# A two-layer hybrid encoder: shares put into the turning matmul, the solve's block products in four lots, the projections in four PSUM banks

## The chip, the core and the metric

The kernel runs on one core of a Trainium2 chip. A core has five engines that work side by side, each on a program of its own that it takes in order: TensorE (PE, matmuls into PSUM), VectorE (DVE), ScalarE (ACT), GpSimd (POOL) and SyncE (SP), which here issues nearly all DMA transfers. PSUM, where matmuls put their sums, has eight banks of 128 partitions x 512 fp32 numbers; all PSUM tiles of this kernel are one or two banks. The metric is device time in microseconds for one call, the median of several runs; lower is better.

## The reference

The input is 512 tokens of 1024 channels. Each of two layers adds half a SwiGLU block (width 2816), a hybrid mixer and another half SwiGLU block to the stream. The mixer projects the normed stream once and feeds three branches: dense attention (4 query heads on 2 key heads, rotary), a mixture of three dilated windows with a learned bias (6 heads; the kernel does it as one softmax with the bias and the logarithm of how many windows hold a key), and a bidirectional gated delta rule (6 heads).

```
def hybrid_mixer(h, rel_bias, w_in, ..., w_out):
    proj = h @ w_in
    aq, ak, av, bq, bk, bv, cq, ck, cv, cz, cb, ca = jnp.split(proj, IN_SPLITS, axis=-1)
    aq = apply_rope(rms_norm(aq, a_qn), cos, sin)          # per head of 64
    ak = apply_rope(rms_norm(ak, a_kn), cos, sin)
    out_a = dense_gqa(aq, ak, av)                          # softmax(q k^T / 8) v
    out_b = dilated_mixture(rms_norm(bq, b_qn), rms_norm(bk, b_kn), bv, rel_bias)
    out_c = gated_deltanet_bidir(cq, ck, cv, cz, cb, ca, c_conv, c_A_log, c_dt_bias, c_out_norm)
    return jnp.concatenate([out_a, out_b, out_c], axis=-1) @ w_out

def gated_delta_chunked(q, k, v, g, beta):                 # chunks of 64 tokens, both directions
    gc = jnp.cumsum(g, axis=-1)
    decay = jnp.where(tril, jnp.exp(gc[..., :, None] - gc[..., None, :]), 0.0)
    M = jnp.where(strict, einsum('bhnid,bhnjd->bhnij', k * beta, k) * decay, 0.0)
    T = triangular_solve(eye + M, eye)                     # one 64x64 inverse per chunk, head, direction
    u, w = T @ (v * beta), T @ (k * beta * jnp.exp(gc))
    a_intra = einsum('bhnid,bhnjd->bhnij', q, k) * decay
    def step(state, xs):                                   # 8 chunks, one after the other
        v_new = u_i - w_i @ state
        o = (q_i * jnp.exp(g_i)) @ state + a_i @ v_new
        state = state * jnp.exp(g_last) + (k_i * jnp.exp(g_last - g_i)).T @ v_new
    ...

def reference(x, ...):
    h = x
    for l in range(DEPTH):                                 # 2
        h = h + 0.5 * swiglu(rms_norm(h, ffn1_norm[l]), ...)
        h = h + hybrid_mixer(rms_norm(h, mix_norm[l]), ...)
        h = h + 0.5 * swiglu(rms_norm(h, ffn2_norm[l]), ...)
    return h
```

In the delta branch q, k and v pass a convolution of five taps and SiLU first, q and k are L2-normed, and the result is normed and multiplied by SiLU(cz).

## The kernel before, in words

**Layout and products.** Channels stand on partitions, the 512 tokens in the free dimension. The large products use fp32r operands split in two: an input `raw` becomes `hi` (rounded, by ScalarE) and `lo` = raw - hi (VectorE), and `mm3` (lines 214 to 218) adds three matmuls, hi by hi, hi by lo, lo by hi. Weights stream from DRAM through two `wraw` buffers; `weight` (line 200) issues the load on SP (line 209), the `whi` copy (210) and the `wlo` subtraction (211).

**Who sets the order.** The source is written as if in sequence. The framework puts all instructions through a scheduler that simulates time and so decides in which order each engine takes its instructions, subject to data, to buffers that must come free, to `issue_after` (this instruction not before that one) and `high_priority`. A pool with `bufs=n` hands out n tiles in turn; a new tile waits for the last reader of the tile whose place it takes. So a change of buffer numbers or of waits moves instructions on every engine.

**The mixer's front** (`mixer`, lines 319 to 366). Two PSUM pools are open while the delta branch is prepared: `mmc` on the right side (three `mm` banks for the projections of q, k and v of the delta branch, `pc`, and one `pss`), and `aux` with four banks on the left for small products: `pR` (line 550, scale rows spread over partitions), `pgq` (614, the 64x64 products of keys and queries per chunk and head) and `pt` (560, 576, transposes; the last reader is the copy to `vs` on ScalarE at 576). Then `aux` and `mmc` close; `join` opens with three banks on the left and `mm` with five on the right (`nmm = 5`), of which four are the former `mmc` banks and one a former `aux` bank. From `mm` come the z projection (`project_z`, 72 matmuls `pc`) and the four group projections (`project_groups`, `pgr`, lines 806 to 808), the group 0 for the dense branch and 1 to 3 for the dilated one. `scales` and `rotate` (from 830 and 858) do the rotary part on VectorE.

**The solve** (`delta_solve`, 623 to 651). The diagonal 32x32 blocks of all 64x64 systems are brought through DRAM into `Z` (96 partitions, both directions; lines 638 and 639, on SP), the reverse direction by way of `zt`. Then 30 rounds r of one multiply into `ztmp` (648) and one add (650) on VectorE, each dependent on the one before. `solve_end` stores the inverses and loads them back into `Y` and `X` (659 to 672). `join_blocks` (683) makes the off-diagonal blocks from them with two sets of 96 matmuls of 32x32 on TensorE, each set in two halves (`pp1`, ScalarE copy `p1s`, `pp2`, four ScalarE copies back to `Y`).

**The attention** (`attention`, from 919) runs in 20 units, five head pairs by four blocks of 128 queries. `scores` of a unit are four matmuls `psc` (954, 955), a row maximum or minimum on VectorE (962, or 966 with the bias), the exponential with its row sum on ScalarE (968, or 963 without the bias), a reciprocal (969) on VectorE, and the multiply by it on GpSimd (970). `weigh` of the unit before (`AHEAD = 1`) turns the probabilities with eight transposes `ppt` (980), copies them on ScalarE (`pth`, 982) and multiplies with v (`pav`, 986). The join is written after the first unit and not issued before its last exponential; then two tables decide: `SCAN_AT` names the units (counted from 0) after which the eight steps of `delta_scan` are written (a step: `pkq`, `prr`, `pS`, `po` on TensorE with VectorE and GpSimd steps between), `FINISH_AT` the unit of `delta_finish`, the output norm of the delta branch (from 1004).

Four lines that the change touches:

```
pt = pp.tile([P, T], F32, name="ppt", tag="t", bufs=2)
for kt in range(NT):
    nc.tensor.transpose(out=pt[:, kt * P:kt * P + P], in_=pb[:, kt * P:kt * P + P], identity=ident)
nc.gpsimd.tensor_tensor(out=pb, in0=pb, in1=sm.to_broadcast([P, T]), op=ALU.mult)
```

Of the kernel before, what the change touches and what calls it, by code (L numbers as in the profile page):

```python
# [9 lines left out]
F32 = mybir.dt.float32  # L10
# [19 lines left out]
SCAN_AT = (1, 3, 4, 6, 7, 9, 10, 12)  # L30
FINISH_AT = 13
# [81 lines left out]
class Body:  # L113
# [205 lines left out]
    def mixer(self, n, l, sm, nxt):  # L319
# [4 lines left out]
        with scope("mix") as mp:  # L324
# [7 lines left out]
            with scope("qkv") as qkvp:  # L332
# [8 lines left out]
                m.nmm = 5  # L341
# [11 lines left out]
                with self.tc.issue_after(m.exps[-1].ins):  # L353
                    m.join_blocks(pool)
                m.square_group(0)
                unit = next(units)
                solve.__exit__(None, None, None)
# [20 lines left out]
class Mixer:  # L378
# [23 lines left out]
    def conv(self, pp, pool, ct):  # L402
# [10 lines left out]
        for j in range(1, 5):  # L413
            nc.vector.scalar_tensor_tensor(out=y, in0=xb[:, j:j + T], scalar=w(j), in1=y, op0=ALU.mult, op1=ALU.add)
# [112 lines left out]
    def delta_keys(self, pool, cs, pss):  # L527
# [16 lines left out]
        nc.vector.tensor_tensor(out=both[32:64], in0=rows[0:32], in1=both[0:32], op=ALU.subtract)  # L544
# [78 lines left out]
    def delta_solve(self, pool):  # L623
# [10 lines left out]
        zt = pool.tile([n96, 32, 32], F32, name="zt", tag="zt")  # L634
# [7 lines left out]
        tmp = pool.tile([n96, 2, 256], F32, name="ztmp", tag="zt")  # L642
# [40 lines left out]
    def join_blocks(self, pool):  # L683
        nc, X = self.nc, self.X
        parts = []
        for hf in range(2):
            for d in range(2):
                a, b = 64 * hf + 32 * d, 64 * hf + 32 * (1 - d)
                parts.append((self.Y[d], slice(a, a + 32), slice(b, b + 32), slice(32 * (1 - d), 32 * (1 - d) + 32)))
        turns = [(q, divmod(q, 6)) for q in range(12)]  # L690
        for tp in range(2):
            p1 = self.aux("pp1")
            for q, (t, h) in turns:
                t += 2 * tp
                for y, ra, rb, cols in parts:
                    nc.tensor.matmul(out=p1[rb, q * 32:q * 32 + 32], lhsT=y[ra, t, h, cols], rhs=X[ra, t * 6 + h],
                                     start=True, stop=True)
            ps = pool.tile([P, 384], F32, name="p1s")
            nc.scalar.activation(out=ps, in_=p1[:, 0:384], func=AF.Copy)
            p2 = self.aux("pp2")  # L700
            for q, (t, h) in turns:
                t += 2 * tp
                for y, ra, rb, cols in parts:
                    nc.tensor.matmul(out=p2[ra, q * 32:q * 32 + 32], lhsT=ps[rb, q * 32:q * 32 + 32],
                                     rhs=y[rb, t, h, cols], start=True, stop=True)
            for y, ra, rb, cols in parts:
                dst = y[ra, 2 * tp:2 * tp + 2].rearrange("p t h i -> p (t h) i")[:, :, cols]
                nc.scalar.activation(out=dst, in_=p2[ra, 0:384].rearrange("p (q i) -> p q i", i=32), func=AF.Copy)
# [210 lines left out]
    def attention(self, ap, pp):  # L919
# [18 lines left out]
        def scores(tile_, t):  # L938
# [18 lines left out]
            for par in range(2):  # L957
# [6 lines left out]
                else:  # L964
# [3 lines left out]
                    nc.scalar.activation(out=pb, in_=pb, func=AF.Exp, scale=-1.0, bias=nm, accum_out=sm)  # L968
                nc.vector.reciprocal(out=sm, in_=sm)  # L969
                nc.gpsimd.tensor_tensor(out=pb, in0=pb, in1=sm.to_broadcast([P, T]), op=ALU.mult)  # L970
                probs.append(pb)
            return probs, state["pv"], v, tile_, t

        def weigh(probs, pv, v, tile_, t):
            tk = slice(t * P, t * P + P)
            turns = []
            for pb in probs:
                pt = pp.tile([P, T], F32, name="ppt", tag="t", bufs=2)
                for kt in range(NT):
                    nc.tensor.transpose(out=pt[:, kt * P:kt * P + P], in_=pb[:, kt * P:kt * P + P], identity=ident)  # L980
                full = ap.tile([P, T], F32, name="pth", bufs=4)
                nc.scalar.activation(out=full, in_=pt, func=AF.Copy)
                turns.append(full)
# [155 lines left out]
```

## Time and profile before

| | |
|---|---|
| median of 3 runs | 2235.09 us (2233.28 to 2237.33) |
| profiled execution, its own time | 2239.25 us |
| its span, first to last instruction | 2237.2 us |
| TensorE matmul (PE), weight loads (PEld) | busy 2168.8 us (97%), 1735.0 us (78%) |
| VectorE (DVE) | 1122.6 us (50%) |
| ScalarE (ACT) | 778.5 us (35%) |
| GpSimd (POOL) | 399.7 us (18%) |
| mean granted clock of TensorE | 0.98 |

The profile is one execution recorded by the hardware. Times are microseconds from the span's start, durations of single instructions in ns where the view says so. A granted clock of 1.00 is the full 2.4 GHz, 0.5 is 1.2 GHz. The two feed-forward blocks of a layer fill TensorE; the mixer of layer 0 lies at about 395 to 713 us, that of layer 1 at about 1505 to 1830. PE's share of 97% overstates how full it is, since a record of a pipelined matmul is longer than the distance to the next one. In a timeline a row is: start, duration, engine, line, operation, output<-inputs, tile, how many in a row, and in brackets the idle time before it with what ended it.

### The profile page before, as it was taken

What the parts mean: (1) busy time and instruction counts of PE and PEld (TensorE: products, weight loads), DVE (VectorE), ACT (ScalarE), POOL (GpSimd) and SP (SyncE); (2) the same over time, 40 slices, a digit from 0 to 9 for tenths busy, and PEclk for the clock granted to TensorE, in tenths of its full rate; (3) what the DMA queues carried; (4) which work ended last, traced back from release to release, by engine and by line L of the source; (5) the groups of instructions that cost most, each with busy time, mean ns of one, the idle gap of its engine ahead of it and who ended that gap; (6) DMA issues with size and microseconds to landing.
All of it is one profiled execution on the core that took longest, in us unless ns stands there. A gap on an engine that the chain in (4) does not pass through costs nothing.

```text
span 2237.2 us, 30694 instructions
## 1 busy us (share of the span) xinstructions
PE 2168.8 (97%) x12548; PEld 1735.0 (78%) x12548; DVE 1122.6 (50%) x1787; ACT 778.5 (35%) x1127; POOL 399.7 (18%) x378
## 2 busy tenths in 40 slices
PE   7999999989898999999999999999898999999999
PEld 5888887769776888888788888877697768888887
DVE  5333334688477543333443333347875765333333
ACT  4222223533565422222332222235336643222221
POOL 3101012210253210101121010123004531101010
PEclk9999999979899999999999999999799999999999
DMA  5332323224202233233322323232242032332323
GB/s 174 124 94 93 96 94 122 78 65 116 77 28 86 85 95 95 94 94 94 94 94 87 102 91 98 92 121 73 74 115 59 28 104 91 95 94 93 97 92 99
DMA packets 93524, 206.83 MB, mean 92 GB/s; under 512 B 38626, under 2 KB 39138, under 8 KB 93385
## 3 DMA queue, kind: packets, MB, share of 16 engines
q1 hardware_dynamic: 91616, 199.98, 29.2%
q10 hardware_dynamic: 1768, 4.91, 0.8%
q8 instruction: 98, 1.61, 0.3%
q14 instruction: 42, 0.34, 0.0%
HBM read 193.83 MB, written 14.18 MB: 93 GB/s over the span
## 4 chain that ended last, share of the span: by engine, by line
PE 88%; DVE 7%; ACT 2%; issue 2%; DMA 1%; POOL 1%; SPq 0%; DVEq 0%; ACTq 0%; POOLq 0%
PE pg L218 15%; PE pg L216 15%; PE pg L217 15%; PE pd L218 7%; PE pd L217 7%; PE pd L216 7%; PE pgr L808 2%; PE pgr L807 2%; PE pgr L806 2%; PE pc L216 2%; PE pc L217 2%; PE pc L218 2%; PE pav L986 1%; PE pwo L217 1%; PE pwo L216 1%
## 5 line engine op out<-in xcount | busy, mean ns | idle before, releaser
L210 ACT ACTIVATE whi<-wraw 128x1024 fp32r<-128x1024 f32 (+3 forms) x344 | 351.4, 1022 | 1234.7 <-PE pg L217 667.1
L216 PE MATMUL pg<-xh,whi 128*128 128x512 f32 x1408 | 557.8, 397 | 8.3 <-ACT xh L236 8.1
L217 PE MATMUL pg<-xl,whi 128*128 128x512 f32 x1408 | 558.3, 397 | 2.9 <-DVE xl L237 2.9
L218 PE MATMUL pg<-xh,wlo 128*128 128x512 f32 x1408 | 557.5, 396 | 0.8 <-DVE wlo L211 0.8
L211 DVE TENSOR_TENSOR wlo<-wraw,whi 128x1024 fp32r<-128x1024 f32 (+3 forms) x344 | 408.1, 1186 | 95.5 <-ACT whi L210 88.3
L296 POOL TENSOR_TENSOR s<-s,rstd 128x512 f32<-128x512 f32 x88 | 152.7, 1737 | 1146.5 <-ACT s L295 1146.5
L216 PEld LDWEIGHTS pg<-xh,whi 128*128 128x128 f32 x1408 | 265.1, 188 | 73.0 <-ACT xh L236 8.1
L217 PEld LDWEIGHTS pg<-xl,whi 128*128 128x128 f32 x1408 | 265.1, 188 | 68.5 <-DVE xl L237 5.2
L218 PEld LDWEIGHTS pg<-xh,wlo 128*128 128x128 f32 x1408 | 265.1, 188 | 65.2 <-DVE wlo L211 1.9
L218 PE MATMUL pd<-hh,wlo 128*128 128x512 f32 x704 | 278.7, 396 | 0.9 <-DVE wlo L211 0.9
L216 PE MATMUL pd<-hh,whi 128*128 128x512 f32 x704 | 278.5, 396 | 0.0
L217 PE MATMUL pd<-hl,whi 128*128 128x512 f32 x704 | 278.4, 395 | 0.0
L310 DVE SCALAR_TENSOR_TENSOR x<-pd,x 128x512 f32<-128x512 f32 x96 | 66.3, 691 | 285.2 <-PE pd L218 285.2
L298 DVE TENSOR_TENSOR h<-pg,s 128x512 f32<-128x512 f32 x88 | 60.9, 692 | 287.6 <-PE pg L218 281.1
L294 DVE TENSOR_TENSOR s<-pg,rstd 128x512 f32<-128x512 f32 x88 | 60.5, 691 | 230.4 <-PE pg L218 230.2
L218 PEld LDWEIGHTS pd<-hh,wlo 128*128 128x128 f32 x704 | 132.3, 188 | 34.0 <-DVE wlo L211 2.2
L217 PEld LDWEIGHTS pd<-hl,whi 128*128 128x128 f32 x704 | 132.4, 188 | 31.8
L216 PEld LDWEIGHTS pd<-hh,whi 128*128 128x128 f32 x704 | 132.4, 188 | 31.8
L970 POOL TENSOR_TENSOR prob<-prob,row 128x512 f32<-128x512 f32 x80 | 82.7, 1040 | 107.2 <-DVE row L969 67.1
L245 POOL TENSOR_TENSOR acc<-acc,sq 128x512 f32<-128x512 f32 x42 | 67.4, 1606 | 132.5 <-ACT sq L244 131.9
L216 PE MATMUL pc<-xh,whi 128*128 128x512 f32 (+1 forms) x208 | 85.4, 412 | 5.6 <-ACT vs L576 4.8
L807 PE MATMUL pgr<-wlo,xh 128*128 128x384 f32 (+1 forms) x256 | 89.9, 351 | 0.0
(248 smaller groups left out, 2554.2 us busy)
## 6 DMA issues: line engine op xcount, KB each, us to landing
wraw<-in_gu_dram SPq DMA_DIRECT2D x176, 512.0 KB, 3.6
wraw<-in_wd_dram SPq DMA_DIRECT2D x64, 448.0 KB, 3.4
wraw<-in_wd_dram SPq DMA_DIRECT2D x32, 512.0 KB, 3.5
wraw<-in_w_c_dram SPq DMA_DIRECT2D x24, 512.0 KB, 3.5
wraw<-in_w_gb_dram SPq DMA_DIRECT2D x24, 384.0 KB, 3.1
wraw<-in_w_o_dram SPq DMA_DIRECT2D x14, 512.0 KB, 4.0
bias<-line SPq DMA_DIRECT2D x12, 448.0 KB, 5.2
saved<-x SPq DMA_DIRECT2D x16, 256.0 KB, 2.0
```

The costliest lines, as they stand in the source:

```text
L210: nc.scalar.activation(out=hi, in_=raw, func=AF.Copy)
L211: nc.vector.tensor_tensor(out=lo, in0=raw, in1=hi, op=ALU.subtract)
L216: nc.tensor.matmul(out=out, lhsT=w[0], rhs=x[0], start=first, stop=False)
L217: nc.tensor.matmul(out=out, lhsT=w[0], rhs=x[1], start=False, stop=False)
L218: nc.tensor.matmul(out=out, lhsT=w[1], rhs=x[0], start=False, stop=last)
L245: nc.gpsimd.tensor_tensor(out=n["acc"], in0=n["acc"], in1=sq, op=ALU.add)
L294: nc.vector.tensor_tensor(out=s, in0=p, in1=n["rstd"], op=ALU.mult)
L296: nc.gpsimd.tensor_tensor(out=s, in0=s, in1=n["rstd"], op=ALU.mult)
L298: nc.vector.tensor_tensor(out=h, in0=pp[1], in1=s, op=ALU.mult)
L310: nc.vector.scalar_tensor_tensor(out=self.x[dm], in0=p, scalar=0.5, in1=self.x[dm], op0=ALU.mult, op1=ALU.add)
L807: nc.tensor.matmul(out=o, lhsT=xh[:, tk], rhs=lo[:, wc], start=False, stop=False)
L970: nc.gpsimd.tensor_tensor(out=pb, in0=pb, in1=sm.to_broadcast([P, T]), op=ALU.mult)
```

## The change

1. *Shares in the turning matmul.* The GpSimd multiply of the probabilities (128x512) by the reciprocal of their sums is gone. VectorE makes instead `share`, the identity (128x128) with its rows multiplied by the reciprocals, and `weigh` uses it as the right operand of a plain fp32 matmul with the unnormed probabilities as the left one. A transpose with the identity becomes a matmul with a diagonal; the product is the transposed block with each column scaled.
2. *The join in four lots.* `join_blocks` takes the indices of lots, one per pair of scan steps (token block t forward, 3 - t backward). Each lot is 24 matmuls, one copy, 24 matmuls and four copies, all in one bank `pp`. Lots 0 and 1 are written after the first unit, 2 and 3 after the second; before, all followed the first. `SCAN_AT` and `FINISH_AT` stand up to one unit earlier.
3. *Projections in their former banks.* `nmm` is 4 instead of 5.
4. *Around the solve.* `zt` lives in the place of the first keys (`kh`) and `ztmp` has its own place (they shared one); the VectorE taps of the convolution of `ct == 7` are not issued before the `rqr` subtraction of `delta_keys`.

```
-SCAN_AT = (1, 3, 4, 6, 7, 9, 10, 12)
-FINISH_AT = 13
+SCAN_AT = (1, 2, 3, 5, 6, 8, 9, 11)
+FINISH_AT = 12
@@ mixer
-                m.nmm = 5
+                m.nmm = 4
...
                 with self.tc.issue_after(m.exps[-1].ins):
-                    m.join_blocks(pool)
+                    m.join_blocks(pool, (0, 1))
                 m.square_group(0)
                 unit = next(units)
+                with self.tc.issue_after(m.exps[-1].ins):
+                    m.join_blocks(pool, (2, 3))
@@ conv
-        for j in range(1, 5):
-            nc.vector.scalar_tensor_tensor(out=y, in0=xb[:, j:j + T], scalar=w(j), in1=y, op0=ALU.mult, op1=ALU.add)
+        with self.tc.issue_after(self.last_r.ins) if ct == 7 else nullcontext():
+            for j in range(1, 5):
+                nc.vector.scalar_tensor_tensor(out=y, in0=xb[:, j:j + T], scalar=w(j), in1=y, op0=ALU.mult, op1=ALU.add)
@@ delta_keys
-        nc.vector.tensor_tensor(out=both[32:64], in0=rows[0:32], in1=both[0:32], op=ALU.subtract)
+        self.last_r = nc.vector.tensor_tensor(out=both[32:64], in0=rows[0:32], in1=both[0:32], op=ALU.subtract)
@@ delta_solve
-        zt = pool.tile([n96, 32, 32], F32, name="zt", tag="zt")
+        zt = self.homes[0].tile([n96, 32, 32], F32, name="zt", tag="kh")
...
-        tmp = pool.tile([n96, 2, 256], F32, name="ztmp", tag="zt")
+        tmp = pool.tile([n96, 2, 256], F32, name="ztmp")
@@ join_blocks
-        for tp in range(2):
-            p1 = self.aux("pp1")
...
+        for lot in lots:
+            parts = []
+            for hf in range(2):
+                for d in range(2):
+                    a, b = 64 * hf + 32 * d, 64 * hf + 32 * (1 - d)
+                    t = lot if d == 0 else 3 - lot
+                    parts.append((self.Y[d][:, t], t * 6, slice(a, a + 32), slice(b, b + 32),
+                                  slice(32 * (1 - d), 32 * (1 - d) + 32)))
+            p = self.aux("pp")
+            for h in range(6):
+                for y, x0, ra, rb, cols in parts:
+                    nc.tensor.matmul(out=p[rb, h * 32:h * 32 + 32], lhsT=y[ra, h, cols], rhs=X[ra, x0 + h],
+                                     start=True, stop=True)
+            ps = pool.tile([P, 192], F32, name="p1s", bufs=2)
+            nc.scalar.activation(out=ps, in_=p[:, 0:192], func=AF.Copy)
...
@@ attention
+                share = ap.tile([P, P], F32, name="share", bufs=2 * AHEAD + 2)
                 nc.vector.reciprocal(out=sm, in_=sm)
-                nc.gpsimd.tensor_tensor(out=pb, in0=pb, in1=sm.to_broadcast([P, T]), op=ALU.mult)
-                probs.append(pb)
+                nc.vector.tensor_scalar(out=share, in0=ident, scalar1=sm, scalar2=None, op0=ALU.mult)
+                probs.append((pb, share))
...
-            for pb in probs:
+            for pb, share in probs:
...
-                    nc.tensor.transpose(out=pt[:, kt * P:kt * P + P], in_=pb[:, kt * P:kt * P + P], identity=ident)
+                    nc.tensor.matmul(out=pt[:, kt * P:kt * P + P], lhsT=pb[:, kt * P:kt * P + P], rhs=share,
+                                     start=True, stop=True)
```

What the scheduler makes of it, at three places. First TensorE's program behind the last convolutions of layer 0 (`pc` is a projection, `pR` and `pgq` as above). Before, the small products follow each other:

```order
L217 MATMUL pc<-xl,whi 128x512
L218 MATMUL pc<-xh,wlo 128x512
L550 MATMUL pR<-rqr,pick 128x512 x6
L614 MATMUL pgq<-kq_3123 64x128 x4
L614 MATMUL pgq<-kq_3124 64x128 x4
L614 MATMUL pgq<-kq_3123 64x128 x2
L614 MATMUL pgq<-kq_3124 64x128 x2
L614 MATMUL pgq<-kq_3125 64x128 x6
```

Now, a few rows further on in the same stretch, the z projection's `pc` stands between them:

```order
L218 MATMUL pc<-xh,wlo 128x512
L553 MATMUL pR<-rqr,pick 128x512
L216 MATMUL pc<-xh,whi 128x512
L217 MATMUL pc<-xl,whi 128x512
L218 MATMUL pc<-xh,wlo 128x512
L216 MATMUL pc<-xh,whi 128x512
L217 MATMUL pc<-xl,whi 128x512
L553 MATMUL pR<-rqr,pick 128x512
L617 MATMUL pgq<-kq_3123 64x128 x4
L218 MATMUL pc<-xh,wlo 128x512
L216 MATMUL pc<-xh,whi 128x512
```

The 72 z matmuls, which came behind all `pR`, `pgq` and `pt`, now stand among the `pR` and `pgq`; the `pt` transposes stand among the matmuls of group 0.

Second, SP's queue at the solve of layer 0 (`w_c` is the weights of the delta branch and z, `w_ga` those of group 0, `w_gb` of groups 1 to 3; `Y` forward is 3169, backward 3170). Before:

```order
L209 DMA wraw<-in_w_c_dram 128x1024 x10
L209 DMA wraw<-in_w_ga_dram 128x1024
L638 DMA s_0_0_3464<-Y_3169 32x24x32 x2
L638 DMA s_0_1_3467<-Y_3170 32x24x32 x4
L638 DMA s_0_0_3464<-Y_3169 32x24x32 x2
L639 DMA zt<-s_0_1_3467 96x1024
L639 DMA Z<-s_0_0_3464 96x1024
L209 DMA wraw<-in_w_ga_dram 128x1024 x3
L209 DMA wraw<-in_w_gb_dram 128x768 x5
L662 DMA s_0_0_3465<-Z 96x1024
```

Now:

```order
L209 DMA wraw<-in_w_c_dram 128x1024 x10
L209 DMA wraw<-in_w_ga_dram 128x1024 x3
L641 DMA s_0_0_3464<-Y_3169 32x24x32 x2
L641 DMA s_0_1_3467<-Y_3170 32x24x32 x3
L209 DMA wraw<-in_w_ga_dram 128x1024
L641 DMA s_0_1_3467<-Y_3170 32x24x32
L641 DMA s_0_0_3464<-Y_3169 32x24x32 x2
L642 DMA Z<-s_0_0_3464 96x1024
L209 DMA wraw<-in_w_gb_dram 128x768
L642 DMA zt<-s_0_1_3467 96x1024
L209 DMA wraw<-in_w_gb_dram 128x768 x11
L665 DMA s_0_0_3465<-Z 96x1024
```

Two more `w_ga` loads stand ahead of the first store of `Y`, one load stands among the stores and one between the loads of `Z` and `zt`; the store of the solved `Z` stands behind the last `w_gb` load instead of the fifth.

Third, GpSimd at the start of layer 0's attention (`prob` the multiply that goes, `qkv` the scaling of the dilated groups, `S` the state of the scan). Before:

```order
L671 COPY bias<-Z 96x512 x2
L881 MEMSET kl_4291 64x512
L970 TENSOR_TENSOR prob<-prob,row 128x512 x8
L855 TENSOR_TENSOR qkv_3968<-qkv_3968,rqb 128x256 x4
L970 TENSOR_TENSOR prob<-prob,row 128x512
L855 TENSOR_TENSOR qkv_4097<-qkv_4097,rqb 128x256 x4
L855 TENSOR_TENSOR qkv_4249<-qkv_4249,rqb 128x256 x4
L970 TENSOR_TENSOR prob<-prob,row 128x512
L763 TENSOR_TENSOR S<-S,lstep 128x384
```

Now:

```order
L674 COPY bias<-Z 96x512 x2
L881 MEMSET kl_4291 64x512
L855 TENSOR_TENSOR qkv_3968<-qkv_3968,rqb 128x256 x4
L855 TENSOR_TENSOR qkv_4097<-qkv_4097,rqb 128x256 x4
L855 TENSOR_TENSOR qkv_4249<-qkv_4249,rqb 128x256 x4
L763 TENSOR_TENSOR S<-S,lstep 128x384 x4
L780 TENSOR_TENSOR otok<-otok,t_5173 64x384 x2
L763 TENSOR_TENSOR S<-S,lstep 128x384
```

The twelve `qkv` scalings follow one another, and nothing stands between the scan's state steps but the outputs of the delta branch, `otok`.

On TensorE the first `prr` of the scan stands behind 24 `psc` matmuls instead of 18, that is twelve score pairs instead of nine, and behind the last `po` there are eight `psc` instead of six.

## Rows read from the trace of the kernel before

**Rows 1.** Stage table of layer 0's mixer, a stretch each.

```profile
core 0: us, PE busy (x) PEld busy (x) DVE busy (x) ACT busy (x) POOL busy (x), PEclk, DMA share, GB/s
...
463.00:494.00 31.00, 24.34 (x139) 17.37 (x140) 23.40 (x61) 11.03 (x13) 0.00 (x0) 0.51 0.33 75
...
494.00:555.00 61.00, 61.00 (x299) 53.96 (x298) 56.55 (x114) 19.35 (x27) 0.00 (x0) 1.00 0.39 103
...
581.00:600.00 19.00, 11.40 (x314) 8.08 (x314) 9.06 (x20) 13.49 (x29) 9.20 (x10) 0.73 0.61 170
600.00:690.00 90.00, 84.52 (x1426) 65.85 (x1423) 63.63 (x151) 58.21 (x121) 47.38 (x53) 0.96 0.06 19
690.00:713.00 23.00, 19.11 (x158) 13.28 (x154) 20.36 (x56) 12.53 (x27) 8.21 (x9) 1.00 0.25 80
```

**Rows 2.** Timeline of TensorE, from the convolutions to the first scores.

```profile
460.87 0.39 PE L217 MATMUL pc<-xl,whi 128*128 128x512 f32 x1
461.10 0.40 PE L218 MATMUL pc<-xh,wlo 128*128 128x512 f32 x1
...
463.39 1.48 PE L550 MATMUL pR<-rqr,pick 64*128 64x512 f32 x3 [1.89 <-DVE rqr L544]
...
488.35 0.80 PE L216 MATMUL pc<-xh,whi 128*128 128x512 f32 x1 [2.38 <-ACT vs L576]
...
507.95 0.86 PE L806 MATMUL pgr<-whi,xh 128*128 128x512 f32 x3
...
580.80 0.34 PE L807 MATMUL pgr<-wlo,xh 128*128 128x384 f32 x1
580.98 0.34 PE L808 MATMUL pgr<-whi,xl 128*128 128x384 f32 x1
```

**Rows 3.** Waits of TensorE: us in total, times, longest.

```profile
PE pc L216 <- ACT vs L576: 4.8, 2, 2.4
...
PE pp L696 <- issue: 4.5, 1, 4.5
```

**Rows 4.** Timeline of VectorE: the solve, and the rotation's end.

```profile
492.39 0.22 DVE L648 TENSOR_TENSOR ztmp<-Z 96x60 f32<-96x60 f32 x1 [7.26 <-DMA Z<-s]
...
537.71 0.27 DVE L650 TENSOR_TENSOR Z<-Z,ztmp 96x60 f32<-96x60 f32 x1
...
554.98 0.56 DVE L874 TENSOR_TENSOR qkv<-qkv,rope 128x384 f32<-128x384 f32 x1
```

**Rows 5.** Turning by source line (min/median/max ns), then TensorE's timeline.

```profile
L980 PE MATMUL ppt<-consts,prob x320: 270/273/474, 589.9 to 1812.1; 128*128 128x128 f32 x160
...
640.99 1.04 PE L980 MATMUL ppt<-consts,prob 128*128 128x128 f32 x8
...
1880.45 1.06 PE L261 MATMUL prow<-consts,rcol 128*128 128x128 f32 x8
```

**Rows 6.** Chains of 581 to 713 and of 640 to 662, by line.

```profile
by line: PE pav L986 10.9%; issue 10.7%; PE ppt L980 8.4%; POOL qkv L855 4.6%; PE psc L954 4.6%; PE psc L955 3.5%; DVE prob L966 3.0%; ACT prob L968 3.0%; DMA woraw<-in_w_o_dram 2.7%; PE pqk L887 2.4%; DVE row L962 2.3%; PE po L769 2.3%; PE
...
614.62 4.88 POOL qkv L855 x8
...
by line: PE pav L986 24.4%; PE ppt L980 15.2%; PE psc L954 13.1%; PE psc L955 9.2%; PE pkq L733 7.8%; PE po L769 6.7%; ACT kh L908 6.2%; PE pS L756 5.8%; PE pqk L887 4.7%; PE prr L746 3.8%; ACT pth L982 2.8%; issue 0.8%
```

**Rows 7.** GpSimd's multiply by source line, and its idle time (us, times).

```profile
L970 POOL TENSOR_TENSOR prob<-prob,row x80: 1029/1040/1062, 585.2 to 1810.5; 128x512 f32<-128x512 f32 x80
...
  DVE row L969: 67.1, 42
```

**Rows 8.** VectorE by source line, all calls: min/median/max ns.

```profile
L426 DVE TENSOR_SCALAR half<-small x2: 178/184/189, 6.3 to 717.3; 128x45 f32<-128x45 f32 x2
...
L812 DVE TENSOR_SCALAR qkv<-pgr,rcol x4: 617/618/618, 580.3 to 1690.8; 128x384 f32<-128x384 f32 x4
```

**Rows 9.** Timeline of TensorE at the mixer's end.

```profile
707.19 0.55 PE L1026 MATMUL pot<-consts,otok 128*128 128x128 f32 x3 [0.94 <-DVE otok L1021]
...
709.86 0.66 PE L1026 MATMUL pot<-consts,otok 128*128 128x128 f32 x4 [0.85 <-DVE z L1030]
```

More of the change, by code (lines that the diff above doesn't have):

```diff
@@ L681, in solve_end, with join_blocks @@
         self.X = X
-    def join_blocks(self, pool):
+    def join_blocks(self, pool, lots):
         nc, X = self.nc, self.X
[L685 to L690, printed above, removed]
-        for tp in range(2):
-            p1 = self.aux("pp1")
[L693 to L696, printed above, removed]
-                                     start=True, stop=True)
[L698 to L708, printed above, removed]
@@ new lines, in join_blocks @@
+        for lot in lots:
[10 more added lines that the diff above has]
+                    nc.tensor.matmul(out=p[rb, h * 32:h * 32 + 32], lhsT=y[ra, h, cols], rhs=X[ra, x0 + h],
+                                     start=True, stop=True)
+            ps = pool.tile([P, 192], F32, name="p1s", bufs=2)
+            nc.scalar.activation(out=ps, in_=p[:, 0:192], func=AF.Copy)
+            for h in range(6):
+                for y, x0, ra, rb, cols in parts:
+                    nc.tensor.matmul(out=p[ra, 192 + h * 32:224 + h * 32], lhsT=ps[rb, h * 32:h * 32 + 32],
+                                     rhs=y[rb, h, cols], start=True, stop=True)
+            for y, x0, ra, rb, cols in parts:
+                nc.scalar.activation(out=y[ra, :, cols], in_=p[ra, 192:384].rearrange("p (h i) -> p h i", i=32), func=AF.Copy)
```

## The prediction

> **What bounds the kernel now.** I read the page first: its slices are dense and at full clock but for one dip in each layer's mixer, where the change lies; then the stage table, the timeline, the waits and the chain. The stage table of layer 0 [rows 1] shows three stretches. From 463 to 494 us TensorE's clock is granted at 0.51, that is the lower of its two levels (1.2 of 2.4 GHz), while VectorE is busy 23.40 of 31 us. From 494 to 581 TensorE is dense. From 581 to 713, the attention with the delta scan, nobody is full: in 600 to 690 VectorE has 63.63 of 90 us, ScalarE 58.21, GpSimd 47.38, and TensorE's 84.52 is flattered, since a record is longer than the distance to the next.
>
> What stands behind the first stretch is in TensorE's timeline [rows 2]. The last matmul of the convolutions starts at 461.10; then come only the `pR`, `pgq` and `pt` products, each waiting for VectorE; the z projection (72 matmuls `pc`) starts at 488.35 after 2.38 us on ScalarE's `vs`; the group projections start at 507.95 and the last stands at 580.98. The list of waits has that `vs` wait twice, once per layer [rows 3]. `vs` is the last reader of a bank of the former `aux` pool, so z waits for a PSUM bank, not for data or weights.
>
> **The mixer's front: banks and the order that follows.** With four `mm` buffers the projections take the four banks that `mmc` leaves. The order of instructions shows the result: in TensorE's program the 72 z matmuls stand among `pR` and `pgq`, and the `pt` transposes among the first group matmuls; before, all of these came first. So z fills the time in which TensorE waited. Count, layer 0, from 461.5 (the last convolution matmul issued) to 581.15 (the first score, one matmul behind 580.98), 119.7 us: z at full clock is 72 x 0.233 = 16.8 us (the spacing 460.87 to 461.10); the groups 507.95 to 581.15 are 73.2 us; `pR`, `pgq`, `pt` took 25.0 us (463.39 to 488.35) with waits and at half clock, so their work is 12.5 us at most, and I put it at 10. Sum 100; at best 119.7 - 100 = 19.7 us per layer go away.
>
> What is late next is VectorE. The solve's chain of 60 dependent multiplies and adds runs 492.39 to 537.98, after an idle 7.26 us on the DMA of `Z`, and the rotation ends at 555.5 [rows 4]: 63 us almost dense. In the new order the solve's steps, the rotation and the weight splits `wlo` of the groups share one stretch, so VectorE again needs about 63 us from the first solve step (z's own steps and three large splits leave the stretch, five smaller ones and the first pair's operands come into it, and I count these as equal). On SP's queue three `w_ga` loads now stand ahead of the stores of Y, one among them, and a `w_gb` load ahead of `zt`. That puts the first step at about 499 instead of 492.4 and the end of the solve at 562; the last split is some 5 us earlier (a dozen short steps follow it), and 4.2 us of matmuls (24 at the 0.175 of 580.80 to 580.98 [rows 2]) follow it: projections end at 561 to 563. So I take 18 of the 19.7 us. Bounds: 20.5 (the three small products at 9 us) and 8 (TensorE still falls to half clock for some 20 us of the stretch, or the split paces it). The solve now ends with the projections instead of 43 us before, so the stores of Z and the loads of Y join the DMA chain of `X` on SP; eight turning matmuls that stood behind the join's first product now stand ahead of it on TensorE and cover that wait. I cost it at nothing, and at 3 us if the cover is too short.
>
> Moving `zt` to the place of the first keys and one convolution's VectorE steps behind `rqr` are in the 18: they are what lets `pR` follow the convolutions without the 1.89 us wait.
>
> **The attention: what the turning costs.** A transpose is one TensorE record: eight in 1.04 us, less the last one's 0.273, are 110 ns each. The new turning is a plain fp32 matmul of 128x128 by 128. That form is in the trace: `prow`, four calls, eight records in 1.06 us, so 112 ns a record and two records a call, 224 ns [rows 5]. 160 turnings a layer cost 160 x (0.224 - 0.110) = 18.2 us more of TensorE. The Trainium skill (TensorE: Matmul & The Clock Gate, section Terms) states that the transpose mode is four times faster for FP32. By that a turning would cost 440 ns and the layer 53 us more; the `prow` rows show twice, not four times, and the sum goes by them.
>
> How much of it counts? The chain through 581 to 713 has 8.4% in `ppt`, that is 11.1 us of 132 [rows 6], out of 160 x 0.110 = 17.6 us of transposes: 63%. So +11.5 us. (In 640 to 662 TensorE's lines sum to 91% of the chain: there all of it counts.)
>
> GpSimd loses 40 multiplies of 1.04 us a layer [rows 7]. On the chain the 4.88 us of `qkv` scaling at 614.62 stand between two of them on its in-order queue; the chain gives 4.6% = 6.1 us to `qkv` [rows 6], and the two multiplies at its ends make 2. These 8.1 us go. What is late next is the same stretch's VectorE work (the `rtb` steps and `vn`), so I credit 5.
>
> VectorE gains 40 `share` products of 128x128 a layer. No row has this form: 45 columns take 184 ns, 384 columns out of PSUM 618 [rows 8]; the line between them gives 290 at 128, and I take that, 11.6 us a layer. Bounds: 7.4 us all hidden (40 x 0.184, zero on the path) and 25 (40 x 0.618). VectorE is busy 70% of this stage but its largest line in the chain has 3.0%; I count a quarter, +3.
>
> The join in four lots keeps its 192 products and its copies' elements; its 4.5 us `issue` gap [rows 3] may go or come back; -1. The scan's first step now stands behind twelve score pairs instead of nine, and its last ahead of four instead of three, so eight steps go with 12 units of attention instead of 14. A step so has 1.5 units beside it instead of 1.75, and a unit's eight turnings cost 0.9 us more: the two about cancel. The final norm starts a unit earlier; before, TensorE waited for it at the end, 0.94 and 0.85 us [rows 9], so -2.
>
> Sum of the attention: 11.5 - 5 + 3 - 1 - 2 = +6.5, taken as +6. Bounds: +18.2 + 11.6 = +30 with no credit, and -8 when GpSimd's and the tail's go in full and the rest hides.
>
> **The sum.** Per layer -18 + 6 = -12, two layers -24 us. The profiled execution took 2239.25 (span 2237.2), the median of the runs is 2235.09; the same 24 off both: 2215 profiled, **2211** as a median.
>
> **Rivals.**
> - *GpSimd was the hidden bound.* 67.1 us of GpSimd's idle time are waits for VectorE's reciprocals [rows 7]: the multiply is a serial link between exponential and turning, 1.04 us each. With it gone the attention shortens by 6 instead of growing: -24 a layer, **2187**. Against it: 640 to 662 is a TensorE chain.
> - *The gap is filled only half.* The clock still falls, or the splits pace TensorE: -9 + 6 = -3 a layer, **2229**. For it: VectorE is busy 23.40 of the 31 us and its splits feed TensorE; against it: z waited for no split.
> - *TensorE becomes the attention's bound.* All 18.2 us count, no credits: 0 a layer, **2235**. For it: 640 to 662; against: the `ppt` share over the whole stage.
> - *Slower: the solve paces everything from SP's queue.* The stores of Y stand behind weight loads that wait for `wraw` buffers, each released a period of 24 x 0.233 = 5.6 us later. If three periods are lost, the solve starts 16.8 us late, and since splits and solve share VectorE the projections end as much later: -18 + 16.8 + 6 = +5 a layer, **2245**. It decides from 12 us of delay. Against it: Y is ready about when the buffers come free.
> - *Slower: the turning at four times a transpose*, a longer matmul in the place of `ppt`: 160 x 0.33 x 0.63 = 33 instead of 11.5 us, -18 + 28 = +10 a layer, **2255**; from 0.32 us a turning the change loses. Against it: `prow`. This is the price that the Trainium skill's section Terms gives.
>
> **How the numbers follow.** Forecast 0.48, hidden GpSimd bound 0.20, half filled 0.10, TensorE bound 0.08, SP's queue 0.10, dear turning 0.04. About 0.2%, 4.5 us, is what a measurement of this kernel can tell from no change. Faster than that: 0.47 + 0.20 + 0.09 + 0.03 = 0.79; within it: 0.07; slower: 0.14. The forecast's own range is 2197 to 2225. For 8 in 10 I go down to 2185 (0.08 lie below) and up to 2242, where about 0.11 lie above.
>
> **What would show it.** Right: z's `pc` records between 461 and 485 at full clock, the `vs` wait gone, the first score near 563; `ppt` with 640 records of 112 ns; `share` near 0.29 us; GpSimd without `prob`; the attention from first score to first dense `pwo` 136 to 142 us. Wrong: a first score later than 573, solve steps starting after 505, a `share` over 0.6 us or a turning over 0.3 us; or an attention shorter than 130 us, which would mean that GpSimd's link was the bound.

## The result, and the profile after

The changed kernel takes 2210.47 us, the median of 4 runs (2208.95 to 2210.93), against 2236.21 before. The ratio is 0.9885, with a 95% interval of [0.9868, 0.9902]; the forecast was 2211. The profiled execution took 2210.73 us with a span of 2208.9, that is 28.3 us less than the span before. The medians are 25.7 us apart: the profiled execution before (2239.25 us) lay 3 us above its median, so what the traces say below holds the difference some 2 to 3 us too large.

First the places to which the prediction was tied, TensorE's timeline of the changed kernel (start, duration, what, idle time before in brackets):

```profile
460.84 0.40 PE L218 MATMUL pc<-xh,wlo 128*128 128x512 f32 x1
461.17 1.19 PE L553 MATMUL pR<-rqr,pick 64*128 64x512 f32 x4
462.29 0.51 PE L216 MATMUL pc<-xh,whi 128*128 128x512 f32 x1
...
560.94 0.34 PE L808 MATMUL pgr<-whi,xl 128*128 128x384 f32 x1
561.12 0.39 PE L954 MATMUL psc<-kh,qs 128*128 128x512 f32 x1
```

`pR` follows the convolutions without the wait of [rows 2], z starts 1.1 us behind the first `pR` instead of 25, and the first score stands at 561.12 instead of 581.15. The stage table of the same kernel, layer 0: the old gap, the solve, the attention up to its last turning, and the attention of layer 1:

```profile
core 0: us, PE busy (x) PEld busy (x) DVE busy (x) ACT busy (x) POOL busy (x), PEclk, DMA share, GB/s
461.00:485.00 24.00, 24.00 (x179) 17.92 (x178) 22.03 (x49) 5.51 (x7) 0.67 (x2) 1.00 0.22 73
503.00:561.00 58.00, 57.49 (x324) 55.52 (x324) 55.47 (x119) 23.88 (x38) 2.70 (x3) 1.00 0.27 79
561.00:692.00 131.00, 125.17 (x2024) 103.37 (x2022) 97.80 (x263) 83.29 (x181) 20.83 (x26) 0.99 0.17 47
1655.00:1787.00 132.00, 125.09 (x2021) 102.60 (x2021) 97.43 (x263) 83.08 (x180) 20.82 (x26) 0.99 0.17 46
```

Against [rows 1], the clock of the old gap is 1.00 where it was 0.51, and TensorE is busy in all of it. The attention's own rows before, over the same stretch of work:

```profile
581.00:713.00 132.00, 115.03 (x1890) 87.20 (x1888) 93.05 (x226) 84.23 (x175) 64.79 (x70) 0.94 0.17 51
1691.00:1823.00 132.00, 117.19 (x1899) 88.40 (x1899) 95.58 (x230) 85.29 (x175) 64.80 (x70) 0.95 0.19 60
```

TensorE was busy for 115 us of 132, with the clock at 0.94; now it is busy for 125 of 131, at 0.99. The waits of TensorE in layer 0's mixer, all that are left (us in total, times, longest):

```profile
PE psc L954 <- ACT prob L963: 3.9, 2, 2.1
PE ppt L981 <- DVE qs L897: 1.9, 2, 1.1
PE pwo L216 <- ACT mxh L1033: 0.8, 1, 0.8
PE pgr L806 <- ACT whi L210: 0.4, 1, 0.4
PE pwo L216 <- DVE x L1051: 0.3, 1, 0.3
PE pwo L217 <- DVE mxl L1034: 0.2, 1, 0.2
```

The `vs` wait and the 4.5 us of `pp` [rows 3] are gone. The chain through the attention of layer 0, that is the work followed back from the last instruction of the stretch, is TensorE's (shares by line, and one of its pieces):

```profile
by line: PE ppt L981 29.5%; PE pav L988 19.1%; PE psc L954 7.6%; PE psc L955 6.0%; PE prr L746 4.6%; PE po L769 4.0%; PE pkq L733 3.3%; PE pS L756 2.9%; DMA woraw<-in_w_o_dram 2.8%; DMA s<-bias 2.4%; DVE qs L897 2.3%; PE pp L699 2.1%; ACT q
...
575.63 0.89 PE ppt L981 x8
```

Compared with [rows 6], the turning went from 8.4% to 29.5%, and `qkv` on GpSimd and `issue` (time in which an engine waits for nothing that the profile shows) are no longer among the large ones. Last, VectorE's timeline with the solve's first step, one of its longest and its last, and the two operations whose price was estimated, by source line (min/median/max ns):

```profile
503.33 0.22 DVE L651 TENSOR_TENSOR ztmp<-Z 96x60 f32<-96x60 f32 x1 [8.30 <-ACT Z L644]
...
541.38 0.59 DVE L651 TENSOR_TENSOR ztmp<-Z 96x420 f32<-96x420 f32 x1
...
559.07 0.27 DVE L653 TENSOR_TENSOR Z<-Z,ztmp 96x60 f32<-96x60 f32 x1
```

```profile
L981 PE MATMUL ppt<-share,prob x640: 270/275/377, 564.6 to 1786.7; 128*128 128x128 f32 x160
...
L971 DVE TENSOR_SCALAR share<-consts,row x80: 275/286/1034, 564.3 to 1783.2; 128x128 f32<-128x128 f32 x80
```

**Where the time went, by layer.** Up to the first score, layer 0 is 20.0 us shorter (561.12 against 581.15). From the first score to the first dense matmul of the feed-forward block the attention is 3.3 us longer (561.12 to 738.43 against 581.15 to 755.18). In layer 1 it is -19.0 (738.43 to 1654.82 against 755.18 to 1690.59, the feed-forward blocks between being the same) and +7.9 (1654.82 to 1833.50 against 1690.59 to 1861.35). Together -28 of the span's -28.3.

### The profile page after: what moved, and what is told of

The parts are those of the page before. It is cut to its first block, busy times and chain, and to the rows that moved or that the text cites. A ratio compares the mean times of both kernels' runs of the same rounds, so it can differ in the third digit from the quotient of the medians.

```text
span 2208.9 us, 31208 instructions
## 1 busy us (share of the span) xinstructions
PE 2174.3 (98%) x12868; PEld 1754.8 (79%) x12868; DVE 1130.1 (51%) x1867; ACT 782.1 (35%) x1147; POOL 320.0 (14%) x298
## 4 chain that ended last, share of the span: by engine, by line
PE 91%; DVE 3%; ACT 2%; DMA 2%; issue 1%; POOL 1%; SPq 0%; ACTq 0%; POOLq 0%; DVEq 0%
PE pg L218 15%; PE pg L216 15%; PE pg L217 15%; PE pd L218 7%; PE pd L216 7%; PE pd L217 7%; PE ppt L981 4%; PE pav L988 2%; PE pgr L807 2%; PE pgr L808 2%; PE pgr L806 2%; PE pc L216 1%; PE pc L218 1%; PE pc L217 1%; PE pwo L218 1%; PE pwo L216 1%
## 5 line engine op out<-in xcount | busy, mean ns | idle before, releaser
L981 PE MATMUL ppt<-share,prob 128*128 128x128 f32 x640 | 91.8, 284 | 3.8 <-DVE qs L897 3.8
L981 PEld LDWEIGHTS ppt<-share,prob 128*128 128x128 f32 x640 | 80.1, 191 | 15.3 <-issue 5.8
L808 PE MATMUL pgr<-whi,xl 128*128 128x384 f32 (+1 forms) x256 | 90.0, 353 | 0.0
```

Of the source, the lines that this page charges most:

```text
L808: mm = nc.tensor.matmul(out=o, lhsT=xl[:, tk], rhs=hi[:, wc], start=False, stop=kk == KD - 1)
L981: nc.tensor.matmul(out=pt[:, kt * P:kt * P + P], lhsT=pb[:, kt * P:kt * P + P], rhs=share, start=True, stop=True)
```

## The experiments

The time of the kernel before differs a little from one set of runs to the next, so all figures below are differences of ratios to the kernel before, times 2237 us; "a layer" is half of that. Each interval reaches about 0.0014 to either side, so a difference of two rows is known to about 2.3 us a layer: those of about 3 us are only just clear of it, and those under 1 us tell nothing.

| run | ratio, 95% interval | against | a layer |
|---|---|---|---|
| the changed kernel | 0.9885 [0.9868, 0.9902] | before | -12.9 us |
| e12_nmm | 0.9877 [0.9863, 0.9891] | before | -13.8 |
| e3_around | 0.9993 [0.9984, 1.0002] | before | -0.8 |
| e1_front | 0.9833 [0.9820, 0.9847] | before | -18.7 |
| e2_turn | 1.0048 [1.0034, 1.0062] | e3_around | +6.2 |
| e5_front_turn | 0.9912 [0.9899, 0.9926] | e1_front | +8.8 |
| e6_front_plain | 0.9966 [0.9953, 0.9979] | e1_front | +14.9 |
| e7_front_nomul | 0.9880 [0.9866, 0.9893] | e1_front | +5.3 |
| e9_nomul_held | 0.9837 [0.9821, 0.9853] | e1_front | +0.4 |
| e8_front_dve | 0.9840 [0.9827, 0.9854] | e1_front | +0.8 |
| e11_dve_held | 0.9873 [0.9857, 0.9889] | e8_front_dve | +3.7 |
| e10_noshare | 0.9911 [0.9898, 0.9925] | the changed kernel | +2.9 |
| e4_back | 0.9861 [0.9847, 0.9874] | the changed kernel | -2.7 |

### The front alone

```
-                m.nmm = 5
+                m.nmm = 4
+ zt in the place of the first keys, ztmp a place of its own,
+ issue_after(self.last_r.ins) around the taps of ct == 7
```

> Before with the front parts alone: four projection banks, the two places around the solve, the one convolution's taps held back. The transposes, GpSimd's multiply, the join in two halves and the scan tables stay. My theory: the first score comes about 20 us earlier in each layer and the attention is what it was before, so 2236 - 2 x 19 = 2198 (2194 to 2204). Rival, the gain is handed back: the solve ends with the projections, and without the join in lots the attention waits for it, 4 or more us a layer, 2206 or more. Rival, the front needs nothing but is lengthened by its own splits: 2215 or more.

Measured 2201.08 us: my theory. The first score is at 561.66, the front 19.5 us shorter, and the attention as before (first score to feed-forward block 174.0 us, before 174.0). Nothing was handed back behind it, and this kernel is 0.5% faster than the changed one.

The two places without the bank (the diff above without its first two lines):

> Before with only the two places around the solve and the one convolution's taps held back; five projection banks. The control of the two runs above. My theory: the 1.9 us wait for the scale rows goes at most, 2232 to 2237, since z still waits for its bank. Rival, these places are what lets the front shorten: 2215 or less.

Measured 2236.06, no change that can be told. And the bank without the two places (the first two lines alone):

> Before with four projection banks and nothing else. My theory, the bank is the cause: most of e1_front's gain, 53 of the 72 z matmuls in the gap against 63 there, 2205 (2201 to 2210). Rival, the moved places around the solve are needed as well: 2215 or more.

Measured 2209.91, at the upper edge of the 2201 to 2210 expected: the bank is the main cause, at -13.8 of the -18.7. The other 5 us a layer come from the places, but only once the bank is there. e12_nmm's timeline shows how:

```profile
462.83 0.40 PE L218 MATMUL pc<-xh,wlo 128*128 128x512 f32 x1
465.12 1.18 PE L550 MATMUL pR<-rqr,pick 64*128 64x512 f32 x4 [1.89 <-DVE rqr L544]
466.44 0.50 PE L216 MATMUL pc<-xh,whi 128*128 128x512 f32 x1
```

The wait of 1.89 us for `rqr` stays, and over the next 25 us the clock is not full in this kernel (465 to 490, then 490 to 511, then the same 25 us in layer 1). The last row is e1_front, without that wait, at 1.00:

```profile
465.00:490.00 25.00, 24.74 (x175) 18.27 (x176) 21.70 (x52) 5.08 (x7) 0.00 (x0) 0.93 0.22 72
490.00:511.00 21.00, 20.88 (x101) 16.70 (x100) 14.53 (x30) 13.50 (x15) 0.00 (x0) 1.00 0.60 138
1559.00:1584.00 25.00, 24.80 (x169) 18.13 (x170) 20.38 (x47) 5.16 (x7) 0.00 (x0) 0.86 0.21 63
...
461.00:486.00 25.00, 25.00 (x184) 18.70 (x183) 23.05 (x52) 6.43 (x8) 0.23 (x1) 1.00 0.24 73
```

In layer 0 the first score of e12_nmm stands 4.8 us behind that of e1_front (566.42 against 561.66): 1.9 us are the wait, and 2.4 us the slower z matmuls, whose distances sum to 20.1 us against 17.7.

### The turning, in its two halves

The diagonal on the kernel before, with the two places for room:

```
-                nc.gpsimd.tensor_tensor(out=pb, in0=pb, in1=sm.to_broadcast([P, T]), op=ALU.mult)
+                nc.vector.tensor_scalar(out=share, in0=ident, scalar1=sm, scalar2=None, op0=ALU.mult)
...
-                    nc.tensor.transpose(out=pt[:, ...], in_=pb[:, ...], identity=ident)
+                    nc.tensor.matmul(out=pt[:, ...], lhsT=pb[:, ...], rhs=share, start=True, stop=True)
```

> Before with the turning by the diagonal of shares and without GpSimd's multiply; the four new buffers do not fit unless the two places around the solve are the new ones too, so these are in it (the run e3_around has them alone). Five projection banks, join and tables of before. My theory: +11.5 - 5 + 3 = +9.5 us a layer, so 2236 + 19 = 2255 (2247 to 2263). Rival, GpSimd's multiply was the bound: -6 a layer, 2224. Rival, TensorE bounds all of the attention: +18 a layer, 2272.

Measured 2248.38, at the lower end of the range. The sign was right; +6.2 against e3_around, where +9.5 was expected. The same on the new front (these lines on top of e1_front's):

> The changed kernel with the join in two halves and the scan tables of before; front and diagonal as changed. If the parts add up: e1_front 2201.1 plus the 12.3 us that the diagonal cost in e2_turn against e3_around, 2213 (2210 to 2217), within 3 us of the changed kernel. Rival, the join in lots pays with the diagonal, since TensorE is then the bound and the lots fill it: 2218 or more. Rival, the join in lots costs, as it seemed to in e4_back against e1_front: 2207 or less.

Measured 2217.35, +8.8 a layer: between the range of the parts adding up, which ends at 2217, and the rival from 2218, by which the join in lots pays with the diagonal. It is not within 3 us of the changed kernel but 3.0 us a layer slower, and that speaks for the rival. TensorE's half alone, with the identity for the diagonal and GpSimd's multiply kept:

```
-                    nc.tensor.transpose(out=pt[:, ...], in_=pb[:, ...], identity=ident)
+                    nc.tensor.matmul(out=pt[:, ...], lhsT=pb[:, ...], rhs=ident, start=True, stop=True)
```

> e1_front with the turning as a plain fp32 matmul with the identity, GpSimd's multiply kept: the price of TensorE's part alone. My term of the sum, 63% of 18.2 us on the path: +11.5 a layer, 2224 (2219 to 2230). Rival, all of it counts: +18.2, 2237. Rival, it fills idle time of TensorE: +6 or less, 2213 or less.

Measured 2229.01: +14.9 a layer, 82% of the 18.2 us and not 63%. The other half, the multiply left out and the transposes kept:

```
-                nc.vector.reciprocal(out=sm, in_=sm)
-                nc.gpsimd.tensor_tensor(out=pb, in0=pb, in1=sm.to_broadcast([P, T]), op=ALU.mult)
```

> e1_front without the multiply on GpSimd and without the reciprocal; the shares are left out of the result. It prices the link that the change takes away. My term: -5 a layer, 2191. By e2_turn, if TensorE's +11.5 and the shares' +3 are right: -8 a layer, 2185. Rival, the link paced the attention: -17 a layer, 2167. Rival, it was hidden: 2199 to 2202.

Measured 2209.92. No theory had it: with 80 multiplies less the kernel is slower, by 5.3 us a layer. In its program the scheduler put the scan behind more score units. Held in its place (with other units in `SCAN_AT` too):

```
+                                m.gates[unit + 5] = m.step_ins     # the first prr of the step just written
...
+            gate = self.gates.get(4 * tile_ + t)
+            with self.tc.issue_after(gate.ins) if gate else nullcontext():
                 for par in range(2):                               # the four psc of a unit
```

> e7_front_nomul with the scan held in its place: the scores of a unit are not issued before the first product of a scan step, so that TensorE's program has the eight steps behind 5.5, 7, 8, 10, 12, 13, 16 and 17 units, as e1_front has (5, 7, 8, 9.5, 12, 13.5, 16, 17.5), and not behind 5.5, 8, 10, 12.5, 14, 16.5, 18 and 20. The shares are left out of the result. Theory, the scheduler's late scan took the gain: -5 a layer against e1_front's 2201, 2191 (2186 to 2196). Rival, GpSimd's multiply was never on the path: 2200 or more.

Measured 2201.50: the late scan explains the 5 us, and beyond that the time is the rival's, since taking the multiply out gains nothing beside transposes. What TensorE waits for instead shows in e9_nomul_held's waits of layer 0's attention, and the clock in its stage rows:

```profile
PE pav L990 <- ACT pth L986: 5.4, 5, 2.0
PE pp L698 <- issue: 4.4, 1, 4.4
PE ppt L984 <- DVE qs L901: 2.0, 1, 2.0
```

```profile
561.00:691.00 130.00, 112.55 (x1878) 86.85 (x1876) 80.01 (x182) 81.68 (x172) 23.19 (x30) 0.92 0.19 54
1653.00:1783.00 130.00, 116.00 (x1894) 89.24 (x1893) 85.35 (x188) 84.65 (x176) 23.21 (x30) 0.92 0.22 59
```

TensorE waits for ScalarE's copy `pth` (1.7 us in e1_front) and runs at 0.92 (e1_front, 562 to 693: 0.95). The end of the attention, which also holds the gain back, comes below with e11_dve_held. VectorE's part of the diagonal, on the changed kernel:

```
-                nc.vector.reciprocal(out=sm, in_=sm)
-                nc.vector.tensor_scalar(out=share, in0=ident, scalar1=sm, scalar2=None, op0=ALU.mult)
...
-                    nc.tensor.matmul(out=pt[:, ...], lhsT=pb[:, ...], rhs=share, start=True, stop=True)
+                    nc.tensor.matmul(out=pt[:, ...], lhsT=pb[:, ...], rhs=ident, start=True, stop=True)
```

> The changed kernel with the identity in the place of the diagonal: no reciprocal, no share on VectorE, the plain matmul stays; the shares are left out of the result. It prices VectorE's part. My term: 3 us a layer, 2212 - 6 = 2206 (2203 to 2209). Rival, hidden beside TensorE: 2210 to 2214. Rival, all 11.4 us of the 40 shares count: 2189.

Measured 2217.40, slower than with the shares by 2.9 us a layer: no theory had it. In layer 0's attention its TensorE waits for the scan's `vn` on VectorE, a wait that the changed kernel doesn't have:

```profile
PE pS L756 <- DVE vn L749: 3.1, 2, 2.7
```

In its program the later scan steps stand up to one unit earlier than in the changed kernel. Leaving instructions out re-orders the rest here, and in e7_front_nomul and this run that moved the time by as much as the terms that were to be priced.

### Undoing the turning, and other places for the multiply

The changed kernel with the four lines of e2_turn's diff taken back:

> The changed kernel with transposes and GpSimd's multiply in the place of the diagonal; everything else as changed. My theory, the turning costs more than GpSimd's multiply: 2210.5 - 19 = 2191 (2184 to 2200), faster than both kernels. Rival, GpSimd's link paces the attention and the matmul turning pays: 2215 to 2222. Rival, the two cancel: 2208 to 2213.

Measured 2206.92: faster than the changed kernel by 2.7 us a layer, under a third of what was expected. It differs from e1_front in the join and the tables alone and is 3.1 us a layer slower, while with the diagonal the same join and tables gain 3.0 (the changed kernel against e5_front_turn). Beside transposes the attention's clock is lower with the lots, 0.92 and 0.93 in the two layers against 0.95 in both in e1_front; whether that is the reason was not tested.

The multiply moved from GpSimd to VectorE, on top of e1_front:

```
-                nc.gpsimd.tensor_tensor(out=pb, in0=pb, in1=sm.to_broadcast([P, T]), op=ALU.mult)
+                nc.vector.tensor_scalar(out=pb, in0=pb, scalar1=sm, scalar2=None, op0=ALU.mult)
```

> e1_front with the multiply of 128x512 on VectorE instead of GpSimd, transposes kept: neither TensorE's extra time nor GpSimd's link. The line through 45 columns at 184 ns and 128 at 286 gives 0.76 us at 512, 30 us a layer on VectorE. My theory: VectorE, busy some 90 of 125 us of the attention, becomes the bound: 2201 to 2215. Rival, VectorE has the room, or does it in half the time, and the shorter link pays: 2185 to 2195.

Measured 2200.39, the same as e1_front: neither theory. The price was far from the line (min/median/max ns):

```profile
L971 DVE TENSOR_SCALAR prob<-prob,row x80: 468/486/1217, 566.6 to 1760.8; 128x512 f32<-128x512 f32 x80
```

0.49 us, not 0.76, and still nothing gained. The scan held earlier, by the gates of e9_nomul_held, with the changed kernel's `SCAN_AT` and `FINISH_AT`:

> e8_front_dve (front, multiply on VectorE, transposes) with the scan held earlier in TensorE's program: steps behind 5.5, 7, 8, 10, 11, 13, 14 and 16 units of attention instead of 5.5, 7.5, 9, 11, 13, 15, 16.5 and 18.5. Theory, the scan and the output norm behind it end the attention: 4 us a layer less, 2192 (2188 to 2197), the fastest of all. Rival, TensorE or VectorE would wait for the scan's short steps instead: 2200 or more.

Measured 2209.48, slower, which is the rival's time but not its reason: TensorE's waits for the scan's steps on VectorE grew only from 4.4 us in e8_front_dve to 6.2, over both layers. The ends of the attention tell more. The last `pav` ends the softmax part, the last `pot` brings in the output of the delta branch, and the last of the output projection comes behind both (us from the first score of the layer, layer 0 and layer 1):

| run | end of the last `pav` | end of the last `pot` |
|---|---|---|
| before | 127.6, 124.3 | 130.9, 127.6 |
| e1_front | 127.5, 124.9 | 130.7, 128.1 |
| e7_front_nomul | 124.2, 120.5 | 139.3, 135.3 |
| e9_nomul_held | 126.9, 120.8 | 134.9, 129.0 |
| e8_front_dve | 123.1, 117.1 | 131.9, 131.6 |
| e11_dve_held | 128.3, 130.8 | 132.6, 134.1 |
| the changed kernel | 133.5, 134.8 | 134.0, 135.4 |

In layer 0 of e7_front_nomul and then of e8_front_dve the last of each stand here:

```profile
684.48 1.09 PE L985 MATMUL pav<-pth,qkv 128*64 128x128 f32 x14 [0.32 <-ACT pth L981]
...
700.04 0.66 PE L1025 MATMUL pot<-consts,otok 128*128 128x128 f32 x4
```

```profile
685.44 1.09 PE L987 MATMUL pav<-pth,qkv 128*64 128x128 f32 x14 [0.69 <-ACT pth L983]
...
694.33 1.05 PE L1027 MATMUL pot<-consts,otok 128*128 128x128 f32 x4
```

With GpSimd's multiply gone or replaced, the softmax part of e7_front_nomul, e9_nomul_held and e8_front_dve ends 0.6 to 7.8 us earlier than in e1_front, and in each of them the delta branch then ends later and last, up to 15 us behind. So the link seems to have been worth something to the softmax part, and the delta branch to have kept the kernel from gaining by it; this is read from the ends, for no run shortened the delta branch alone. e11_dve_held does not settle whether an earlier scan would pay: with the scores made to wait for the scan, the last `pav` came 5.3 and 13.7 us later than in e8_front_dve and the last `pot` hardly moved. How far the attention of the kernels with transposes, 168 to 178 us from the first score to the feed-forward block, can be shortened at this end is open.

## Why the prediction was right, and where its terms were not

**The front, -18 forecast, -20.0 and -19.0 in the trace.** Right in the mechanism: the bank was the wait, and z filled the gap. The count of work (100 us) came out almost exactly, with a little luck: from 461.17 to 561.12 are 99.95 us, in which TensorE waits 0.4 us; by the distances of its records the three small products took 7.7 us and not 10, and z (17.7 instead of 16.8), the groups, some turning matmuls and the wait took as much more. So all 19.7 us went and not 18: VectorE was not late next. The solve started at 503.3 rather than 499, but from its first to its last step VectorE needed 56 us and not 63, so it ended at 559.3 rather than 562; the last split came 5 us ahead of that, as expected, and the projections end with the solve. The solve's first step came 10.9 us later than before, behind ScalarE's copy into `Z`, which in turn came behind the DMA of `zt`; that is just short of the 12 from which the rival of SP's queue was to decide, and it cost no time. The edits around the solve were put into the 18 together with the bank; e12_nmm against e1_front shows them to be 5 of it.

**The attention, +6 forecast, +3.3 and +7.9 in the trace.** Right in the sum, but by offsets, and that is luck: its terms were mis-sized in both directions.

- *TensorE, +11.5: measured +14.9* (e6_front_plain). The spacing was right: eight `ppt` records in 0.89 us of the chain, 0.111 each. What failed is the share of the old chain, 63%, as the measure of how much counts: a line that grows takes over the chain, and `ppt` stands in it afterwards with 29.5% of 131 us, 38.6 us. That is all of its 320 x 0.112 = 35.8, and more, since many of its pieces of eight stand in the chain with 1.09 us.
- *GpSimd's link, -5, and the shares, +3.* Neither is a price by itself. Next to transposes, taking the link out is worth nothing (e9_nomul_held) or costs 5.3 (e7_front_nomul); next to the plain matmul, link and shares together are worth -6.0 (e5_front_turn against e6_front_plain) instead of -2. There TensorE's waits before the scores (`psc`) fall from 13.0 us over both layers to 4.6. The `share` itself took 286 ns, with 290 estimated, and that is luck too: the line went through a row that reads PSUM, and the like line misses by far at 512 columns (e8_front_dve).
- *Join, -1: measured -3.0* (the changed kernel against e5_front_turn), though +3.1 next to transposes. TensorE's waits before `pp` are 6.2 us over both layers in e5_front_turn and 1.1 in the changed kernel, which is 2.5 of the 3.0 a layer.
- *Norm, -2.* TensorE's waits at `pot`, 4.3 us over both layers before, are gone, but already in e6_front_plain and e5_front_turn, which have the old tables: with the longer turning TensorE itself comes to `pot` later, and the gain is part of the +14.9. Here the tables do nothing: with the old `SCAN_AT` and `FINISH_AT` the changed kernel's instructions come in the same order on every engine. What moved the scan is the scheduler's own clock, fed by the other edits.

14.9 - 6.0 - 3.0 = +5.9, against 11.5 - 5 + 3 - 1 - 2 = +6.5. The three measured steps lead from e1_front to the changed kernel by way of e6_front_plain and e5_front_turn, so they must add up; in another order each step has another price (the diagonal with link and shares: +8.8 with the old join, +2.7 with the lots).

Two figures beside the sum were off in the working itself: GpSimd's 8.1 and the tail's 2 make a lower bound of -10 and not -8, and with 63% counting the change loses from 0.34 us a turning and not 0.32.

**Rivals.** TensorE did become the attention's bound, as one rival had it, but the layer did not come out at 0 as that rival said. Part of the reason may be the clock: the denser TensorE also ran at the full level more of the time, 0.99 against 0.94 over some 131 us. With a full and a half level, a mean of 0.94 means 12% of the time at half rate and 0.99 means 2%, so some 13 us a layer at half rate are gone, worth up to 6 or 7 us. Over this stretch the kernels with transposes have 0.90 to 0.97, those with plain matmuls 0.94 to 1.00. In e6_front_plain, layer 0 stayed at 0.94 (e1_front 0.95) and its attention grew by 16.4 us; layer 1 rose to 0.98 (e1_front 0.95) and grew by 11.8. How much of the offset this is was not separated by a run. GpSimd as the hidden bound is not borne out: no run without its multiply beats e1_front. The half-filled gap is refuted by the clock of 1.00, the dear turning by two records of 0.111 us. The Trainium skill's fourfold (TensorE: Matmul & The Clock Gate, section Terms) does not agree with this trace, where it is twofold. From first score to last `pot`, behind which the output projection is dense, the attention took 134.0 us in layer 0 and 135.4 in layer 1 (before 130.9 and 127.6), just below the 136 that I named.

## What to carry to other kernels

Where an engine waits for a place and not for data, count the work in the stretch: the sum of spacings at full clock is what is left when the wait goes, and it held here to 1 us. A line's share of the old chain was a poor price in both directions: of the turning, which grew, 82% counted and not 63%, and the link, 8.1 us by the chain, gained nothing when it was taken out beside transposes, where the delta branch ended last. So price a line that grows near its full work, and for a line that shrinks look up which chain ends next. Where a scheduler sets the order, a part alone may have another sign than within the whole, so the best version is found by leaving parts out: the front alone, at 0.9833, beats the whole change.

## What the runs showed that was not expected

The fp32 multiply of 128x512 by a column took 486 ns on VectorE and 1040 on GpSimd. From 128 columns (286 ns) to 512 that is 0.52 ns a column, under half of the 1.2 ns that lie between the 45 columns of [rows 8] and 128. The solve's multiplies of two fp32 tensors, 0.22 us at 60 columns and 0.59 at 420 in the changed kernel, come to 1.03 ns a column. The Trainium skill (VectorE: DVE Perf Modes, section The perf-mode tier table) has fp32 `tensor_scalar` within SBUF at twice the base rate, which agrees if 1.03 ns is taken as the base.
